# Probabilities times values with v's low part in the columns that held zeros

## The chip, the cores and the metric

The kernel runs on one core of a Trainium2 chip. The metric is the device time of one launch in microseconds. The engines in the profile are PE (matrix products; PEld is its weight load), DVE (vector), ACT (scalar), POOL and SP (which here issues DMAs).

## What is computed

Two layers of an encoder over 256 tokens of width 1024, one batch entry, float32. Each layer is a mixer with three kinds of attention heads of width 64 side by side, and then a gated feed-forward part:

```python
def mixer_sublayer(x, n1, w_in_l, qg, kg, rpb_l, og, w_out_l, tables):
    h = rms_norm(x, n1)
    proj = h @ w_in_l
    qa, ka, va, qd, kd, vd, qc, kc, vc = jnp.split(proj, cuts, axis=-1)
    ...                       # norms of q and k, rotations
    out_a = neighbourhood_attention(qa, ka, heads(va, H_NA), rpb_l, na_idx, na_dr, na_dc)   # 4 heads
    out_d = dilated_window_attention(qd, kd, heads(vd, H_DIL), dil_idx, dil_val)            # 6 heads
    out_c = gqa_block_attention(qc, kc, heads(vc, H_GKV))                                   # 6 heads on 2 of k, v
    mix = jnp.concatenate([rms_norm(out_a, og[:NA_W]), rms_norm(out_d, ...), rms_norm(out_c, ...)], axis=-1)
    return x + mix @ w_out_l

def channel_sublayer(x, n2, w_gu, cw, cb, w_dn):
    h = rms_norm(x, n2)
    g, u = jnp.split(h @ w_gu, 2, axis=-1)
    g = depthwise_conv_centred(g, cw, cb)
    return x + (jax.nn.gelu(g, approximate=False) * u) @ w_dn
```

The change is in the step of every attention that multiplies the probabilities, 256 queries by 256 keys, with the values v of the head.

## The kernel before

**Number format.** Every matrix product runs on float32r operands, which keep fewer digits than float32. So each operand is split: its high part is the rounded value, its low part the difference, and a product is the sum of three, high by high, high by low and low by high (`mm3`). For a weight, ACT writes `wp_hi` by a cast and DVE writes `wp_lo` by a subtraction, in chunks of 512 columns (`split`).

**Order of the work.** The program does not issue instructions as it is written. `Plan` records each operation with its tiles, `order()` puts them in one order with a list scheduler (an operation's start from its engine, its inputs and the buffer slots that it needs, by a table of costs and of handovers between engines; ties by the place in the program, shifted by `later`), and `emit()` issues them. So every instruction carries line 413 in the profile, and what is read are the names of the tiles. Each engine runs its own list in order. A changed operation changes the lists of all engines.

**Stages of a layer.** First come the norm and transposes of x (`act_hT`), then the projections into `psa` banks, split into seven pieces (`dq`, `dk`, `dv`, `cq`, `ckv`, `aqk`, `av`). The attention handles the heads in pairs: `scores` writes the scores of two heads, `softens` the softmax (DVE adds the bias and takes the maximum, ACT the exponential and the scaling), `turn` transposes the probabilities on PE and splits them into `act_ch` (high, by ACT) and `act_cl` (low, by DVE), and `weigh` multiplies them with v into a PSUM bank `psw_w`. `mixed` scales a finished pair into `act_mixT_hi` and `act_mixT_lo` and squares it into `act_sqm`; `group_rstd` turns the squares of a group of heads into the factor of its norm. The remaining projections, and the output projections of the groups that are ready, are a stock of products (`filler`) with which PE fills the waits of the attention. The output projections of the last group, of the residual into `const_x`, and the norm and transposes for the feed-forward part end the mixer. The feed-forward part is 11 steps of products with a fixed order.

**Values before.** Tiles `vown` and `vkv` exist twice, for v's high and low part. Each has the heads at odd places of 64 columns and zeros, written once by POOL, at the even places. The slice for a head is 128 columns, its own 64 and 64 zeros, before them or behind them by whether the head is even or odd (`beside_zeros`). So the product of a head gives 128 rows, of which the 64 of the other head of the pair are zero, and both heads of a pair are summed into one bank of 128 x 256: even heads in the lower 64 partitions, odd heads in the upper ones. Per head there are two key halves of three products:

```python
                for kt in range(NT):
                    mm3(
                        op, self.v[0][:, kt], self.v[1][:, kt], hi[:, kt], lo[:, kt],
                        first and kt == 0, last and kt == NT - 1,
                    )
```

`values_of` writes the high part with one ACT instruction and the low part with one DVE instruction per 128 tokens.

Of the kernel before, what the change touches and what calls it, by code (L numbers as in the profile page):

```python
# [455 lines left out]
def encoder_kernel(  # L456
# [70 lines left out]
    with nc.later(1000):  # L527
# [288 lines left out]
    for l in range(DEPTH):  # L816
# [163 lines left out]

        def values(places, src, t):

            hi, lo = places
# [4 lines left out]
        def values_of(tiles, ps, c0, t, nh):  # L988
            src = ps[:, c0 : c0 + nh * HD].rearrange("p (h d) -> p h d", d=HD)
            values([z[:, t, 1 : 2 * nh : 2] for z in tiles], src, t)  # L990

        def beside_zeros(tiles, h, odd):

            i = 2 * h + 1 - odd
            return [z[:, :, i : i + 2].rearrange("p t m d -> p t (m d)") for z in tiles]


        class Head:
# [103 lines left out]
        def prep_c(which, g):  # L1102
# [4 lines left out]
            for t in range(NT):  # L1107
# [4 lines left out]
                if which == "k":  # L1112
# [3 lines left out]
                    )  # L1116
                    values_of(vkv, ps, GKV_W, t, H_GKV)
                hold["c" + which, t] = z
# [50 lines left out]
        for h in range(H_DIL):  # L1169
            heads.append(Head("d", h, h, [dil[:, t] for t in range(NT)], beside_zeros(vown, h, h % 2)))  # L1170
        for h in range(H_GQ):
            kv = h // (H_GQ // H_GKV)
            heads.append(Head("c", h, kv, None, beside_zeros(vkv, kv, h % 2)))
        for h in range(H_NA):
            heads.append(Head("a", h, h, na_bias(h), beside_zeros(vown, h, h % 2)))

        def values_a():
            for t in range(NT):
                values_of(vown, pj["av"][t], 0, t, H_NA)
# [22 lines left out]
        for t in range(NT):  # L1202
            values_of(vown, pj["dv"][t], 0, t, H_DIL)
        wv.fill(1500)
# [241 lines left out]
```

## Time and profile before

| | before |
|---|---|
| time, median of 3 runs (lowest to highest) | 617.32 us (617.11 to 617.4) |
| profiled execution, span from first to last instruction | 615.5 us |
| busy share of the span: PE, DVE, ACT, POOL | 98%, 79%, 70%, 14% |
| value products (`act_ch` and `act_cl` by `const_v`) | 192 |
| additions and copies across partitions | none |

The page gives the profiled execution's span and no other time of it; the median of the runs lies 1.8 us above the span. A row of a group or of the timeline gives engine, operation, output tile, input tiles and shape; "x88 | 36.8, 422" means 88 instructions, 36.8 us busy together, 422 ns the mean of one. Durations of neighbours on an engine overlap, so the distance from start to start is often shorter than a duration. A number in brackets at the end of a timeline row is the idle time of the engine ahead of it, and what ended it.

### The profile page before, as it was taken

What the parts mean: (1) busy time and instruction counts of PE and PEld (TensorE: products, weight loads), DVE (VectorE), ACT (ScalarE), POOL (GpSimd) and SP (SyncE); (2) the same over time, 40 slices, a digit from 0 to 9 for tenths busy, and PEclk for the clock granted to TensorE, in tenths of its full rate; (3) what the DMA queues carried; (4) which work ended last, traced back from release to release, by engine and by line L of the source; (5) the groups of instructions that cost most, each with busy time, mean ns of one, the idle gap of its engine ahead of it and who ended that gap; (6) DMA issues with size and microseconds to landing.
All of it is one profiled execution on the core that took longest, in us unless ns stands there. A gap on an engine that the chain in (4) does not pass through costs nothing.

```text
span 615.5 us, 9869 instructions
## 1 busy us (share of the span) xinstructions
PE 604.9 (98%) x3484; PEld 523.7 (85%) x3484; DVE 486.9 (79%) x1000; ACT 428.3 (70%) x1064; POOL 84.0 (14%) x136
## 2 busy tenths in 40 slices
PE   8999999999999999999999999998999999999997
PEld 7998878888888888888899988887888888888885
DVE  4888989888778988878867797867877777777774
ACT  6888989686566677666588898866755656556651
POOL 2741230212400000000032213333000000000000
PEclk9999999999999999999999999999999999999999
DMA  8894313656596999988445644554565566555501
GB/s 287 275 291 143 102 35 104 208 192 195 164 252 235 364 353 325 309 278 269 154 150 173 222 137 171 205 175 135 179 231 171 176 204 205 166 180 201 185 21 68
DMA packets 85073, 121.44 MB, mean 197 GB/s; under 512 B 9864, under 2 KB 69608, under 8 KB 85024
## 3 DMA queue, kind: packets, MB, share of 16 engines
q1 hardware_dynamic: 82752, 112.17, 55.6%
q0 software_dynamic: 1728, 8.39, 4.0%
q8 instruction: 27, 0.44, 0.3%
q10 hardware_dynamic: 544, 0.26, 0.2%
q14 instruction: 22, 0.18, 0.1%
HBM read 110.93 MB, written 9.88 MB: 196 GB/s over the span
## 4 chain that ended last, share of the span: by engine, by line
PE 92%; DVE 3%; ACT 2%; issue 1%; DMA 1%; POOL 0%; SPq 0%; DVEq 0%; ACTq 0%
PE psw_w L413 49%; PE psa_a L413 43%; DVE const_x L413 1%; ACT act_s2k L413 1%; DVE wp_lo L413 1%; DMA wp_raw<-in_w_in_dram 1%; DVE act_hT L413 1%; ACT act_hT L413 1%; ACT wp_hi L413 1%; POOL small_rstd L413 0%; ACT act_mixT_hi L413 0%; POOL small_ms L413 0%; SPq L413 0%; DVE act_mixT_lo L413 0%; DVE small_ss L413 0%
## 5 line engine op out<-in xcount | busy, mean ns | idle before, releaser
L413 DVE TENSOR_TENSOR wp_lo<-wp_raw,wp_hi 128x512 fp32r<-128x512 f32 (+2 forms) x332 | 232.3, 731 | 42.9 <-ACT wp_hi L413 41.4
L413 PE MATMUL psw_w<-act_hT,wp_hi 128*128 128x512 f32 x704 | 247.8, 397 | 2.1 <-DVE act_hT L413 2.1
L413 ACT CAST wp_hi<-wp_raw 128x512 fp32r<-128x512 f32 (+2 forms) x332 | 203.1, 662 | 26.1 <-PE psw_w L413 15.3
L413 PE MATMUL psw_w<-act_hT,wp_lo 128*128 128x256 f32 x704 | 196.1, 279 | 0.1
L413 PEld LDWEIGHTS psw_w<-act_hT,wp_hi 128*128 128x128 f32 x704 | 131.9, 188 | 34.1 <-DVE act_hT L413 3.0
L413 PEld LDWEIGHTS psw_w<-act_hT,wp_lo 128*128 128x128 f32 x704 | 132.6, 188 | 1.5 <-DVE wp_lo L413 0.4
L413 PE MATMUL psa_a<-wp_hi,act_hT 128*128 128x384 f32 (+2 forms) x448 | 112.8, 332 | 0.7 <-ACT act_hT L413 0.5
L413 ACT COPY act_s2k<-psw_w 128x256 f32<-128x256 f32 x88 | 32.4, 373 | 76.3 <-PE psw_w L413 76.3
L413 PEld LDWEIGHTS psa_a<-wp_hi,act_hT 128*128 128x128 f32 x448 | 77.9, 189 | 3.8 <-ACT act_hT L413 1.0
L413 PE MATMUL psa_a<-wp_lo,act_hT 128*128 128x384 f32 (+2 forms) x224 | 74.7, 334 | 0.0
L413 PE MATMUL psa_a<-wp_lo,act_ch 128*128 128x512 f32 x176 | 69.5, 395 | 0.0
L413 PE MATMUL psa_a<-wp_hi,act_ch 128*128 128x512 f32 x176 | 69.4, 394 | 0.0
L413 PE MATMUL psa_a<-wp_hi,act_cl 128*128 128x512 f32 x176 | 65.8, 394 | 0.0
L413 DVE TENSOR_TENSOR act_s2k<-psw_w,act_s2k 128x256 f32<-128x256 f32 x88 | 36.8, 422 | 31.1 <-ACT act_s2k L413 30.7
L413 PEld LDWEIGHTS psa_a<-wp_lo,act_hT 128*128 128x128 f32 x224 | 42.3, 189 | 2.0 <-DVE wp_lo L413 1.0
L413 PEld LDWEIGHTS psa_a<-wp_hi,act_ch 128*128 128x128 f32 x176 | 33.1, 188 | 7.9
L413 PEld LDWEIGHTS psa_a<-wp_hi,act_cl 128*128 128x128 f32 x176 | 33.2, 188 | 7.8
L413 PEld LDWEIGHTS psa_a<-wp_lo,act_ch 128*128 128x128 f32 x176 | 33.1, 188 | 6.9
L413 DVE SCALAR_TENSOR_TENSOR act_s2k<-act_s2k,act_cw,act_s2k 128x255 f32<-128x255 f32 x88 | 36.9, 478 | 1.5 <-ACT act_s2k L413 1.3
L413 POOL TENSOR_TENSOR small_rstd<-small_ms,const_mh 128x6 f32<-128x6 f32 (+2 forms) x26 | 31.6, 1216 | 2.2
L413 ACT ACTIVATE act_s2k<-act_s2k,act_cw 128x256 f32<-128x256 f32 x44 | 24.1, 595 | 9.8 <-DVE act_s2k L413 9.4
L413 PE MATMUL psw_w<-act_ch,const_v 128*128 128x256 f32 x128 | 28.6, 286 | 1.1 <-ACT act_s2k L413 1.1
(112 smaller groups left out, 779.3 us busy)
## 6 DMA issues: line engine op xcount, KB each, us to landing
wp_raw<-in_w_gate_up_dram SPq DMA_DIRECT2D x44, 1024.0 KB, 5.1
wp_raw<-in_w_down_dram SPq DMA_DIRECT2D x22, 1024.0 KB, 4.8
wp_raw<-in_w_in_dram SPq DMA_DIRECT2D x14, 768.0 KB, 5.3
wp_raw<-in_w_in_dram SPq DMA_DIRECT2D x8, 1024.0 KB, 6.3
wp_raw<-in_w_out_dram SPq DMA_DIRECT2D x8, 768.0 KB, 6.4
dram_khi<-act_mixT_hi SPq DMA_DIRECT2D x4, 768.0 KB, 4.3
dram_klo<-act_mixT_lo SPq DMA_DIRECT2D x4, 768.0 KB, 5.6
wp_lo<-dram_klo POOLq DMA_DIRECT2D x4, 768.0 KB, 4.8
```

The lines of the kernel that those rows point to most:

```text
L413: getattr(o.engine.real, o.method)(*map(real, o.args), **{k: real(v) for k, v in o.kw.items()})
```

## The change

v's high and low part now stand side by side in one tile. In `vown` two heads take four places of 64 columns, high, low, low, high; an even head's slice is [high, low], an odd head's [low, high]. In `vkv` each of the two heads takes three places, high, low, high, so that a slice of either kind can be taken. One product of the probabilities' high part and one of their low part with the 128 columns then give the product with v's high part in one half of the partitions and that with v's low part in the other half. Two products per key half take the place of three; the product of low by low, which was left out, is now included. The two heads of a pair have a half bank of 256 columns each. `mixed` adds the halves: ACT copies the half that lies in the other 64 partitions to where it belongs (`act_mxs`), DVE adds it to the half that lies there already (`act_mxm`), for each head of the pair. What followed reads the sum from SBUF instead of the bank, and POOL takes the squares of all pairs of a group but the last. The low parts of `vown` are written with two DVE instructions instead of one, and the high part of `vkv` is written twice by one ACT instruction of double width. The zeros and their four memsets go.

```diff
-    vown, vkv = (
-        [const.tile([P, NT, 2 * n + 1, HD], F32R, tag=f"v{n}{i}", name=f"v{n}{i}") for i in range(2)]
-        for n in (H_DIL, H_GKV)
-    )
-    for z in vown + vkv:
-        nc.gpsimd.memset(z[:, :, 0::2].bitcast(F32), 0.0)
+    vown = const.tile([P, NT, 2 * H_DIL, HD], F32R, tag="vown", name="vown")
+    vkv = const.tile([P, NT, 3 * H_GKV, HD], F32R, tag="vkv", name="vkv")
...
+        def values_own(ps, t, nh):
+            z = vown[:, t, : 2 * nh].rearrange("p (h m) d -> p h m d", m=4)
+            hi, lo = z[:, :, 0:4:3], z[:, :, 1:3]
+            src = ps[:, : nh * HD].rearrange("p (h e d) -> p h e d", e=2, d=HD)
             r = rx[:, t : t + 1]
             nc.scalar.activation(hi, src, AF.Copy, scale=r)
-            nc.vector.scalar_tensor_tensor(lo, src, r, hi.bitcast(F32), ALU.mult, ALU.subtract)
+            for e in range(2):
+                nc.vector.scalar_tensor_tensor(
+                    lo[:, :, e], src[:, :, e], r, hi[:, :, e].bitcast(F32), ALU.mult, ALU.subtract
+                )
...
-            def weigh(self, op, first, last):
-                hi, lo = self.pT
+            def weigh(self, op):
                 for kt in range(NT):
-                    mm3(
-                        op, self.v[0][:, kt], self.v[1][:, kt], hi[:, kt], lo[:, kt],
-                        first and kt == 0, last and kt == NT - 1,
-                    )
+                    for i, z in enumerate(self.pT):
+                        nc.tensor.matmul(
+                            op, self.v[:, kt], z[:, kt],
+                            start=kt == 0 and i == 0, stop=kt == NT - 1 and i == 1,
+                        )
 
         def mixed(op, gi, i):
...
-            nc.scalar.activation(h, op, AF.Copy, scale=g)
-            nc.vector.scalar_tensor_tensor(mixT_lo[:, k], op, g, h.bitcast(F32), ALU.mult, ALU.subtract)
+            small_ = act.tile([P, S], F32, tag="mxs", name=f"mxs{gi}{l}{i}", bufs=1)
+            m = act.tile([P, S], F32, tag="mxm", name=f"mxm{gi}{l}{i}", bufs=2)
+            for e, (mine, other) in enumerate(((LOW, HIGH), (HIGH, LOW))):
+                nc.scalar.copy(small_[mine], op[other, e])
+            for e, mine in enumerate((LOW, HIGH)):
+                nc.vector.tensor_tensor(m[mine], op[mine, e], small_[mine], op=ALU.add)
+            nc.scalar.activation(h, m, AF.Copy, scale=g)
+            nc.vector.scalar_tensor_tensor(mixT_lo[:, k], m, g, h.bitcast(F32), ALU.mult, ALU.subtract)
             sq = act.tile([P, S], F32, tag="sqm", name=f"sqm{gi}{l}{i}", bufs=2)
-            nc.scalar.activation(sq, op, AF.Square)
+            if i < n - 1:
+                nc.gpsimd.tensor_tensor(sq, m, m, op=ALU.mult)
+            else:
+                nc.scalar.activation(sq, m, AF.Square)
...
         def weigh(i):
             gi, h = groups[i]
             if h % 2 == 0:
-                hold["op"] = psw.tile([P, S], F32, tag="w", name=f"o_{l}{i}")
-            heads[i].weigh(hold["op"], h % 2 == 0, h % 2 == 1)
+                hold["op"] = psw.tile([P, 2, S], F32, tag="w", name=f"o_{l}{i}")
+            heads[i].weigh(hold["op"][:, h % 2])
```

More of the change, by code (lines that the diff above doesn't have):

```diff
@@ L979, in by_pairs, with values_kv, both_parts @@
             return both
-        def values(places, src, t):
-            hi, lo = places
+        def values_own(ps, t, nh):
+            z = vown[:, t, : 2 * nh].rearrange("p (h m) d -> p h m d", m=4)
+            hi, lo = z[:, :, 0:4:3], z[:, :, 1:3]
+            src = ps[:, : nh * HD].rearrange("p (h e d) -> p h e d", e=2, d=HD)
             r = rx[:, t : t + 1]
             nc.scalar.activation(hi, src, AF.Copy, scale=r)
-            nc.vector.scalar_tensor_tensor(lo, src, r, hi.bitcast(F32), ALU.mult, ALU.subtract)
[L988 to L995, printed above, removed]
+            for e in range(2):
+                nc.vector.scalar_tensor_tensor(
+                    lo[:, :, e], src[:, :, e], r, hi[:, :, e].bitcast(F32), ALU.mult, ALU.subtract
+                )
+        def values_kv(ps, c0, t):
+            z = vkv[:, t].rearrange("p (h m) d -> p h m d", m=3)
+            src = ps[:, c0 : c0 + H_GKV * HD].rearrange("p (h d) -> p h d", d=HD)
+            r = rx[:, t : t + 1]
+            nc.scalar.activation(
+                z[:, :, 0:3:2], src.unsqueeze(2).to_broadcast([P, H_GKV, 2, HD]), AF.Copy, scale=r
+            )
+            nc.vector.scalar_tensor_tensor(z[:, :, 1], src, r, z[:, :, 0].bitcast(F32), ALU.mult, ALU.subtract)
+        def both_parts(z, i):
+            return z[:, :, i : i + 2].rearrange("p t m d -> p t (m d)")
         class Head:
@@ L1169, in encoder_kernel @@
         for h in range(H_DIL):
-            heads.append(Head("d", h, h, [dil[:, t] for t in range(NT)], beside_zeros(vown, h, h % 2)))
+            heads.append(Head("d", h, h, [dil[:, t] for t in range(NT)], both_parts(vown, 2 * h)))
         for h in range(H_GQ):
             kv = h // (H_GQ // H_GKV)
-            heads.append(Head("c", h, kv, None, beside_zeros(vkv, kv, h % 2)))
+            heads.append(Head("c", h, kv, None, both_parts(vkv, 3 * kv + h % 2)))
         for h in range(H_NA):
-            heads.append(Head("a", h, h, na_bias(h), beside_zeros(vown, h, h % 2)))
+            heads.append(Head("a", h, h, na_bias(h), both_parts(vown, 2 * h)))
         def values_a():
             for t in range(NT):
-                values_of(vown, pj["av"][t], 0, t, H_NA)
+                values_own(pj["av"][t], t, H_NA)
         groups = [(gi, h) for gi, n in enumerate((H_DIL, H_GQ, H_NA)) for h in range(n)]
@@ L1202, in encoder_kernel @@
         for t in range(NT):
-            values_of(vown, pj["dv"][t], 0, t, H_DIL)
+            values_own(pj["dv"][t], t, H_DIL)
         wv.fill(1500)
```

3 lines of the change are left out of this document (2 added, 1 removed).

## Prediction

> **What bounds the kernel now.** I read the first part of the page, then the windows cut at the stages, then the timeline of one stretch of probability-times-value products, then the groups by form, and the chain of waits for the seams between stages.
>
> ```profile
> span 615.5 us, 9869 instructions
> PE 604.9 (98%) x3484; PEld 523.7 (85%) x3484; DVE 486.9 (79%) x1000; ACT 428.3 (70%) x1064; POOL 84.0 (14%) x136
> PE 92%; DVE 3%; ACT 2%; issue 1%; DMA 1%; POOL 0%; SPq 0%; DVEq 0%; ACTq 0%
> ```
>
> PE is busy nearly throughout and carries 92% of the chain that ended last, so a matmul taken out should be time won. But shares over the whole span hide stages. In the next view the columns are PE, PEld, DVE, ACT and POOL busy (instructions), granted clock, DMA share, GB/s. The first two rows are layer 0 from the first scores to the last value product, and from there to the feed-forward part; the fourth and fifth are the same two stages of layer 1.
>
> ```profile
> 45.00:114.50 69.50, 68.01 (x491) 59.51 (x491) 62.03 (x175) 61.27 (x181) 15.01 (x20) 1.00 0.32 107
> 114.50:127.70 13.20, 12.07 (x65) 9.42 (x63) 11.35 (x22) 10.67 (x26) 4.31 (x6) 1.00 0.54 172
> 127.70:311.60 183.90, 183.89 (x971) 156.78 (x972) 151.56 (x258) 120.61 (x225) 9.52 (x18) 1.00 0.79 261
> 346.70:412.30 65.60, 65.04 (x479) 57.38 (x479) 52.76 (x159) 55.78 (x168) 19.07 (x29) 1.00 0.48 164
> 412.30:429.10 16.80, 15.11 (x78) 11.90 (x76) 11.81 (x22) 10.35 (x26) 4.87 (x8) 1.00 0.39 131
> ```
>
> The change touches the first, second, fourth and fifth rows only. The feed-forward stages are PE alone. In the attention of layer 0, DVE is busy 62.03/69.50 = 89% and ACT 88%; in layer 1, 80% and 85%. PE is kept full there because projection and output-projection products fill the waits of the softmax; those fillers are a fixed stock. The clock is 1.00 everywhere and stays out of the sum.
>
> **What it removes.** Each head goes from six products of 256 columns to four; 16 heads and two layers make 192 into 128. The timeline of PE gives the distance from one to the next:
>
> ```profile
> 101.92 0.40 PE L413 MATMUL psw_w<-act_ch,const_v 128*128 128x256 f32 x2
> 102.15 0.28 PE L413 MATMUL psw_w<-act_cl,const_v 128*128 128x256 f32 x1
> 102.27 0.40 PE L413 MATMUL psw_w<-act_ch,const_v 128*128 128x256 f32 x2
> 102.50 0.28 PE L413 MATMUL psw_w<-act_cl,const_v 128*128 128x256 f32 x1
> 102.62 0.40 PE L413 MATMUL psw_w<-act_ch,const_v 128*128 128x256 f32 x2
> 102.86 0.28 PE L413 MATMUL psw_w<-act_cl,const_v 128*128 128x256 f32 x1
> 102.98 0.28 PE L413 MATMUL psw_w<-act_ch,const_v 128*128 128x256 f32 x1
> ```
>
> Nine products start between 101.92 and 102.98: 1.06/9 = 0.118 us each (the 0.28 us of one is overlapped). 64 x 0.118 = 7.55 us off PE, 3.8 a layer, with their weight loads inside. The four memsets of zeros on POOL go too, in the first microseconds, with nobody waiting for them: nothing.
>
> **What it adds.** For each of eight pairs of heads a layer: two ACT copies and two DVE additions of 64x256, since one half of the result lies in the other 64 partitions. No row has 64 partitions; the nearest are the same operations on 128.
>
> ```profile
> L413 DVE TENSOR_TENSOR act_s2k<-psw_w,act_s2k 128x256 f32<-128x256 f32 x88 | 36.8, 422 | 31.1 <-ACT act_s2k L413 30.7
> L413 ACT COPY act_s2k<-psw_w 128x256 f32<-128x256 f32 x88 | 32.4, 373 | 76.3 <-PE psw_w L413 76.3
> L413 ACT ACTIVATE act_sqm<-psw_w 128x256 f32<-128x256 f32 x16 | 6.2, 388 | 0.0
> L413 DVE SCALAR_TENSOR_TENSOR const_v<-psa_a,small_rx,const_v 128x384 fp32r<-128x384 f32 x4 | 2.4, 612 | 0.5 <-ACT const_v L413 0.5
> L413 DVE SCALAR_TENSOR_TENSOR const_v<-psa_a,small_rx,const_v 128x256 fp32r<-128x256 f32 x4 | 1.7, 471 | 0.0
> L413 DVE SCALAR_TENSOR_TENSOR const_v<-psa_a,small_rx,const_v 128x128 fp32r<-128x128 f32 x4 | 1.3, 345 | 0.0
> 96.58 0.42 DVE L413 CUSTOM_DVE_ANT_0 act_s2k<-psw_w,act_nab 128x256 f32<-128x256 f32 x1
> 96.92 0.42 DVE L413 CUSTOM_DVE_ANT_0 act_s2k<-psw_w,act_nab 128x256 f32<-128x256 f32 x1
> ```
>
> An addition costs DVE between 0.34 (the two custom operations of the same width start 96.58 and 96.92) and 36.8/88 = 0.42 us. The values' low part is written in two instructions for one, four more a layer: two of 128 columns for one of 256 are 2 x 345 - 471 = 0.22 us more, and 384 split in two about the same by interpolation, 0.9 a layer at most, 0.5 if the ends overlap. DVE gains 16 x 0.34 + 0.5 = 5.9 to 16 x 0.42 + 0.9 = 7.6 us a layer. I take 6.7, the middle, since DVE queues are full there but not always. ACT gains 16 x 32.4/88 = 5.9 and loses five squares of 0.39 to POOL: 4.0 net, and some 0.3 for writing the grouped values' high part twice. POOL gets five squares a layer; its sum of squares over two tiles takes 0.74, and POOL is idle three quarters of the stage. The low part of the mixed result is computed from SBUF rather than PSUM, at the same width: nothing.
>
> **Where it lies, layer 0.** The PE gain would shorten the 69.5 us to 65.7. DVE then has 62.0 + 6.7 = 68.7 us of work for it, which doesn't fit. At 69.5 us unchanged it would be 99% full. What allows that at all is that part of its 7.5 us idle is stall that ends: the mixed low part waits for ACT's square on the same PSUM bank, which the new order of reads removes for most pairs.
>
> ```profile
> L413 DVE SCALAR_TENSOR_TENSOR act_mixT_lo<-psw_w,const_gains,act_mixT_hi 128x256 fp32r<-128x256 f32 x16 | 7.6, 476 | 4.3 <-ACT act_sqm L413 3.0 <-ACT act_mixT_hi L413 1.3
> 114.54 0.48 ACT L413 ACTIVATE act_mixT_hi<-psw_w,const_gains 128x256 fp32r<-128x256 f32 x1 [2.26 <-PE psw_w L413]
> 117.49 0.72 POOL L413 TENSOR_SCALAR small_ms<-small_ss 128x2 f32<-128x2 f32 x1 [1.38 <-DVE small_ss L413]
> ```
>
> Against it stand the new waits: an addition waits for ACT's copy, and behind it on DVE stand low parts of weights and of turned probabilities (act_cl), which PE's fillers and value products wait for. So I put the attention of layer 0 at no change, DVE having taken over from PE as what ends last. The seam behind it (114.5 to 127.7) is a chain from the last product over mixed result, squares, group norm, residual, transposes to the feed-forward part; before its 114.54 now come two copies and two additions, 2 x 0.37 + 2 x 0.42 = 1.6 us with every handover on top, less what overlaps (the second copy runs under the first addition): 1.3. In the changed kernel's PE order 25 output-projection products stand behind the last value product, for 29 before, so PE is no longer what fills it. DVE's wait for POOL and the weight splits in that seam can take half of the 1.3: +0.6 for layer 0.
>
> **Layer 1.** Here the order says the most: 23 such products stand behind the last value product, for 41. Their distance is read off the chain of waits:
>
> ```profile
> 412.35 3.97 PE psa_a L413 x17
> ```
>
> 3.97/17 = 0.234 us, so 18 x 0.234 = 4.2 us of filler have moved from the seam into the attention, in place of the 3.8 removed. The attention stays at 65.6 us, with DVE at 52.8 + 6.7 = 59.5 (91%), and the seam shrinks: not by 4.2, since the chain that took 13.2 us in layer 0, now 1.3 longer, bounds it at 14.5: 16.8 - 14.5 = 2.3 gained.
>
> Sum: +0.6 - 2.3 = -1.7 us, made on the profiled span, 615.5 to 613.8. The page gives no other time for that execution; the median of the runs shown, 617.32, is 1.8 above the span, and I keep that difference: 615.6.
>
> **A rule against it.** POOL's new squares read SBUF while DVE subtracts weights in SBUF. The trace has the case:
>
> ```profile
> 83.31 0.73 POOL L413 TENSOR_TENSOR act_sqm<-act_sqm,act_sqm 128x256 f32<-128x256 f32 x1
> 83.65 0.68 DVE L413 TENSOR_TENSOR act_z<-act_z,act_gna 128x256 f32<-128x256 f32 x1
> 85.90 0.41 DVE L413 TENSOR_TENSOR act_z<-act_z,act_gna 128x256 f32<-128x256 f32 x1
> ```
>
> The same operation takes 0.68 under POOL's and 0.41 alone: 0.27 us for each square that meets one, 1.4 a layer at most; it is priced in the slower rival. [...]
>
> **Rivals.** (1) *Held additions.* If a DVE instruction that starts at the other 64 partitions lets the one before it drain, the addition on the upper half and the instruction behind it each lose the overlap of 0.42 - 0.34 = 0.08 us: two instructions for each of eight pairs, 16 x 0.08 = 1.3 us in layer 0, where DVE is the bound, and hidden in layer 1: 616.9. No row has a start at another partition, for or against. [...]
>
> (2) *DVE bounds layer 0 outright: slower.* It runs in order and waits for ACT, PE and POOL. The fullest stretch of over ten microseconds that I found is early in layer 1's attention:
>
> ```profile
> 353.30:366.00 12.70, 12.70 (x85) 10.67 (x86) 11.99 (x37) 11.96 (x33) 1.94 (x4) 1.00 0.36 115
> ```
>
> That is 11.99/12.70 = 94%. With the work of 68.7 and 1.4 of contention at that share, the stage takes 74.6, 5.1 us more; with the seam's +0.6 to 1.3 and layer 1's -2.3, +3.4 to 4.1: about 621. It decides from the share where the loss in layer 0 eats the 2.3, that is 70.1/(69.5 + 1.7) = 98% with contention, 96% without. For it: both DVE and ACT near 90%, in-order queues, only one filler product of the four early units left at the end of layer 0. Against: the square's stall goes, and DVE's queue holds weight splits that fill its waits.
>
> (3) *PE stays the bound in both layers: the full gain.* DVE additions at 0.34, seams covered: 617.3 - 7.5 + 1.2 for two seams = 611.0. For it: 98% PE. Against: 62.0 + 5.9 in 65.7 us is 103%.
>
> That the change does not do what it says I set aside: the built order has 64 fewer products on PE, 32 additions on DVE and 32 copies on ACT more.
>
> **How the numbers follow.** The forecast, 615.6 with its own range 613.5 to 617, gets 0.38; (1) 616.9, 0.15; (2) 621, 0.31; (3) 611, 0.16. Range 610.8 to 621.5: from the full gain to (2) with a margin for its share. What a measurement here can tell from no change is 0.2%, 1.2 us: faster means under 616.1, slower over 618.6. Faster: 0.31 of the forecast, 0.16 of (3), 0.01 of (1) = 0.48. Same: 0.07 + 0.11 = 0.18. Slower: 0.31 + 0.03 = 0.34.
>
> **What would show it.** Right: the 128x256 value products 128 with 0.118 between them; DVE over 95% in the attention of layer 0, PE with new idle there released by DVE or ACT; the seam of layer 1 two microseconds shorter, that of layer 0 not. An addition under 0.34 or over 0.45 breaks the price. Wrong: PE idle of several microseconds in layer 0's attention (rival 2), or both attentions 3 us shorter (rival 3).

## The result, and the profile after

The changed kernel takes 627.25 us (median of 4 runs, 625.93 to 627.67), the kernel before beside it 617.36 us (617.11 to 618.11): the ratio is 1.0158, 95% interval 1.0146 to 1.0171. It is 9.9 us slower, where 1.7 us faster was forecast. The profiled execution has a span of 625.2 us, 9.7 above that of before, so the traces can be compared stage by stage. First the head of the page after: span, engines, and the chain that ended last.

```profile
span 625.2 us, 9798 instructions
PE 606.1 (97%) x3420; PEld 517.1 (83%) x3420; DVE 502.7 (80%) x1040; ACT 439.9 (70%) x1086; POOL 92.4 (15%) x142
PE 82%; DVE 7%; ACT 7%; POOL 2%; issue 1%; ACTq 0%; POOLq 0%
```

PE has 64 instructions fewer and carries ten points less of the chain; DVE and ACT carry 14% of it instead of 5%. DVE gained 15.8 us of work and ACT 11.6. The windows cut at the same stages as before: attention and seam of layer 0, its feed-forward part, attention and seam of layer 1. The columns are PE, PEld, DVE, ACT and POOL busy (instructions), granted clock, DMA share, GB/s.

```profile
45.10:119.60 74.50, 70.36 (x463) 57.63 (x463) 67.70 (x190) 66.22 (x190) 19.23 (x26) 0.98 0.30 100
119.60:135.90 16.30, 12.22 (x62) 8.51 (x60) 15.15 (x29) 12.51 (x30) 6.24 (x6) 1.00 0.48 171
135.90:319.80 183.90, 183.90 (x971) 156.74 (x972) 150.67 (x256) 119.58 (x223) 10.95 (x19) 1.00 0.78 259
354.80:423.90 69.10, 67.11 (x465) 56.76 (x465) 59.68 (x177) 60.36 (x177) 23.66 (x36) 1.00 0.49 168
423.90:438.80 14.90, 11.12 (x60) 8.28 (x59) 11.45 (x23) 11.31 (x28) 4.18 (x6) 1.00 0.31 97
```

The feed-forward row is the same to a tenth. The attention of layer 0 went from 69.5 to 74.5 us and its seam from 13.2 to 16.3; the attention of layer 1 from 65.6 to 69.1 and its seam from 16.8 to 14.9. That is +5.0, +3.1, +3.5 and -1.9, together +9.7: all of the difference. The 0.98 in the first row is a stretch of 3.4 us in which PE had half its clock (last section); that can be up to some 1.7 of the 5.0. PE's longest waits from the start of layer 0's attention to the end of its seam (engine, what it waited for, us in total, times, longest) name DVE and ACT. First all of the kernel before, then the four longest of the changed one, whose waits there sum to 7.9 us:

```profile
PE psw_w L413 <- ACT act_s2k L413: 1.1, 1, 1.1
PE psw_w L413 <- DVE act_mixT_lo L413: 0.4, 1, 0.4
```

```profile
PE psw_w L413 <- DVE act_hT L413: 2.5, 2, 1.4
PE psw_w L413 <- ACT act_s2k L413: 1.6, 2, 0.8
PE psw_w L413 <- DVE const_x L413: 1.3, 2, 1.0
PE psa_a L413 <- DVE wp_lo L413: 1.1, 3, 0.6
```

The groups show what the added operations cost:

```profile
L413 DVE TENSOR_TENSOR act_mxm<-psw_w,act_mxs 64x256 f32<-64x256 f32 x32 | 13.4, 418 | 2.6 <-ACT act_mxs L413 2.2
L413 ACT COPY act_mxs<-psw_w 64x256 f32<-64x256 f32 x32 | 11.8, 367 | 7.5 <-PE psw_w L413 6.6 <-DVE act_mxm L413 0.3
L413 DVE SCALAR_TENSOR_TENSOR act_mixT_lo<-act_mxm,const_gains,act_mixT_hi 128x256 fp32r<-128x256 f32 x16 | 8.1, 509 | 2.8 <-ACT act_mixT_hi L413 2.8
L413 POOL TENSOR_TENSOR act_sqm<-act_mxm 128x256 f32<-128x256 f32 x10 | 6.8, 676 | 36.3 <-DVE act_mxm L413 36.3
```

An addition took 0.418 us and a copy 0.367, both as priced. The mixed result's low part took 0.509 instead of 0.476. So the single prices held. Their sum was too small: over the whole kernel DVE gained 15.8 us of busy time where 13.4 were forecast, ACT 11.6 where 8.6 were. The next sections show that the place where they fall was read wrong as well.

### The profile page after: what moved, and what is told of

Read it like the earlier page. It is cut to its first block, busy times and chain, and to the rows that moved or that the text cites. A ratio compares the mean times of both kernels' runs of the same rounds, so it can differ in the third digit from the quotient of the medians.

```text
span 625.2 us, 9798 instructions
## 1 busy us (share of the span) xinstructions
PE 606.1 (97%) x3420; PEld 517.1 (83%) x3420; DVE 502.7 (80%) x1040; ACT 439.9 (70%) x1086; POOL 92.4 (15%) x142
## 4 chain that ended last, share of the span: by engine, by line
PE 82%; DVE 7%; ACT 7%; POOL 2%; issue 1%; ACTq 0%; POOLq 0%
PE psw_w L413 46%; PE psa_a L413 37%; ACT act_s2k L413 3%; DVE wp_lo L413 2%; ACT wp_hi L413 1%; POOL small_rstd L413 1%; DVE const_x L413 1%; DVE act_mxm L413 1%; ACT act_mxs L413 1%; DVE act_cl L413 1%; ACT act_hT L413 1%; DVE act_mixT_lo L413 1%; DVE small_nm L413 1%; ACT act_ch L413 0%; DVE small_ss L413 0%
## 5 line engine op out<-in xcount | busy, mean ns | idle before, releaser
L413 PE MATMUL psa_a<-wp_lo,act_ch 128*128 128x512 f32 x176 | 69.5, 395 | 0.0
L413 POOL TENSOR_TENSOR small_s1x<-small_ssx 128x2 f32<-128x2 f32 x4 | 4.9, 1218 | 176.6 <-ACT act_s2k L413 176.6
```

Source lines behind the costliest of these rows:

```text
L413: getattr(o.engine.real, o.method)(*map(real, o.args), **{k: real(v) for k, v in o.kw.items()})
```

## The experiments

Times below are medians; a ratio is against the kernel before beside it, with its 95% interval. A difference between two changed kernels is worked out from their ratios, times 617.4 us, with the two half-widths added in squares. Most of these kernels have stretches of 3.4 us in which PE had half its clock (last section), and not the same number in each execution. In the profiled executions a mean granted clock of 0.999 or 1.00 goes with none in the stages that matter (the kernel before has 1.000), 0.997 with one (the changed kernel) and 0.994 with two (the kernel with one more ACT copy); for the executions without a profile the number is estimated from their mean clock in the same way. Where it decides a reading, executions of equal clock are compared as well; that is one to six executions on a side.

The first theory was that the copies and additions load DVE and ACT beyond what the attention can hide; its rival that the order which the scheduler writes anew for the shorter products loses the time. The first four kernels split the change.

**The products alone.** The bank of a pair is used as it stands; copies, additions and POOL's squares go.

```diff
-            ...                                        # two copies, two additions
+            m = op[:, 0]
-            if i < n - 1:
-                nc.gpsimd.tensor_tensor(sq, m, m, op=ALU.mult)
-            else:
-                nc.scalar.activation(sq, m, AF.Square)
+            nc.scalar.activation(sq, m, AF.Square)
```

> Leaves out the copies and additions of the halves: the mixed result is read from one head's half bank, as the kernel before reads its bank, with ACT's squares; the two products per key half stay. If the additions are the whole loss (theory D: DVE, and ACT with it, bound layer 0 and the seams), the PE gain comes through: 64 x 0.118 = 7.5 us less than before, about 610 to 612. If the fixed stock of fillers hides PE's gain anyway (theory F), 615 to 617. If something of the new value layout or of the rewritten order costs by itself (theory O), 617 or more.

Measured 615.25 us, ratio 0.9978 (0.9966 to 0.9990): 1.4 us faster. 7.5 us of work left PE and 1.4 arrived; in the six of ten executions without a stretch at half clock, 615.1 us, it was 2.3.

**The copies and additions alone**, put into the mixed step of the kernel before, with its three products and zeros. POOL's squares come with them.

```diff
-            nc.scalar.activation(h, op, AF.Copy, scale=g)
-            nc.vector.scalar_tensor_tensor(mixT_lo[:, k], op, g, h.bitcast(F32), ALU.mult, ALU.subtract)
...
+            for e, (mine, other) in enumerate(((LOW, HIGH), (HIGH, LOW))):
+                nc.scalar.copy(small_[mine], op[other])
+            for e, mine in enumerate((LOW, HIGH)):
+                nc.vector.tensor_tensor(m[mine], op[mine], small_[mine], op=ALU.add)
+            nc.scalar.activation(h, m, AF.Copy, scale=g)
+            nc.vector.scalar_tensor_tensor(mixT_lo[:, k], m, g, h.bitcast(F32), ALU.mult, ALU.subtract)
...
```

> The kernel before, three products and zeros, with the changed kernel's copies, additions and POOL squares put in its mixed step (it adds the other head's rows to each, so the sum is not the reference's). Theory D: the loss is that of the additions, and PE was no longer the bound in layer 0, so taking the products away bought little: 628 to 632. If the gain of 7.5 was won in full and merely outweighed (theory S, plain sum of +17 and -7.5): 634 to 636.

Measured 629.38 us, 1.0198 (1.0181 to 1.0215): 12.2 us slower. With the additions present, going from three products to two is worth 2.5 us (629.38 to the changed kernel, by the ratios); without them 1.4. So two things are to be explained: why additions of 0.42 us cost 12 us, and why 7.5 us off PE are worth so little in either case.

**Additions and copies over all 128 partitions**, so that no instruction starts at another partition than the one before it. The order of instructions is the changed kernel's on every engine; the values are not, since each half bank is added to its own copy.

```diff
-            for e, (mine, other) in enumerate(((LOW, HIGH), (HIGH, LOW))):
-                nc.scalar.copy(small_[mine], op[other, e])
-            for e, mine in enumerate((LOW, HIGH)):
-                nc.vector.tensor_tensor(m[mine], op[mine, e], small_[mine], op=ALU.add)
+            for e in range(2):
+                nc.scalar.copy(small_[:, e], op[:, e])
+            for e in range(2):
+                nc.vector.tensor_tensor(m2[:, e], op[:, e], small_[:, e], op=ALU.add)
```

> The changed kernel with copies and additions of the same number and the same 256 columns, but over all 128 partitions of each half bank, so that no instruction starts at another partition than its neighbours (the sum of a half with its own copy, not with the other half). Theory Hd (an addition at the upper 64 partitions and its successor are held until DVE has drained): neighbouring additions start 0.34 apart instead of 0.43 to 0.46, DVE has 16 x 0.1 = 1.6 us less a layer, and the time falls by 1.5 to 3 us, to 624 to 626. If holding costs nothing, 627.

Measured 623.16 us, 1.0091 (1.0073 to 1.0108): 4.1 us (2.8 to 5.4) less than the changed kernel. The timelines of DVE and of ACT, changed kernel first, then this one, show the same pair of additions and the same pair of copies:

```profile
71.68 0.86 DVE L413 TENSOR_TENSOR act_mxm<-psw_w,act_mxs 64x256 f32<-64x256 f32 x2
70.90 0.75 ACT L413 COPY act_mxs<-psw_w 64x256 f32<-64x256 f32 x2
```

```profile
70.82 0.74 DVE L413 TENSOR_TENSOR act_mxm<-psw_w,act_mxs 128x256 f32<-128x256 f32 x2
70.02 0.65 ACT L413 COPY act_mxs<-psw_w 128x256 f32<-128x256 f32 x2
```

With 0.42 us for one, the second starts 0.43 us after the first in the changed kernel, when that has ended, and 0.32 after it here, 0.10 before its end. Where the two additions of a pair stand apart in the changed kernel, the rows show that it is the start that holds, and not the 64 partitions:

```profile
84.32 0.40 DVE L413 TENSOR_TENSOR act_mxm<-psw_w,act_mxs 64x256 f32<-64x256 f32 x1
84.64 0.41 DVE L413 TENSOR_TENSOR act_z<-act_z,act_gna 128x256 f32<-128x256 f32 x1
85.08 0.43 DVE L413 TENSOR_TENSOR act_mxm<-psw_w,act_mxs 64x256 f32<-64x256 f32 x1
85.54 0.69 DVE L413 TENSOR_TENSOR act_cl<-psw_w,act_ch 128x512 fp32r<-128x512 f32 x1
```

Behind the lower addition, the first of a pair, the next instruction starts after 0.32 us, 0.08 before its end. The upper one starts 0.44 us behind an instruction of 0.41, and what follows it 0.46 us later, where it takes 0.43: both start 0.03 us behind the end of the one before, both are held. ACT shows the same: with 0.37 us for one copy, the second starts 0.38 us after the first in the changed kernel, and 0.27 after it here, where one takes 0.38. So the 4.1 us are what holding costs on DVE and ACT together, and this experiment does not part the two. A little of it is the clock: at equal clock the difference is 3.5 to 3.9.

**The squares back on ACT.**

```diff
-            if i < n - 1:
-                nc.gpsimd.tensor_tensor(sq, m, m, op=ALU.mult)
-            else:
-                nc.scalar.activation(sq, m, AF.Square)
+            nc.scalar.activation(sq, m, AF.Square)
```

> The changed kernel with all squares on ACT. Theory P (POOL's squares slow DVE's subtractions in SBUF and are slowed by them, 0.3 to 0.5 each): 1 to 3 us faster, 624 to 626. If ACT, 89% busy in layer 0, is what bounds, ten more squares of 0.31 make it 1 to 3 us slower, 628 to 630.

Measured 629.44 us, 1.0203 (1.0179 to 1.0226), 2.8 us (1.2 to 4.4) more than the changed kernel: ten squares on ACT cost more than what DVE may lose beside POOL's squares (in the kernel before one DVE operation took 0.68 us beside a sum of squares and 0.41 alone). What DVE loses to them over the kernel is not measured by itself. Of the 2.8, some is the clock: the four executions have 0.989 to 0.997, and the one at 0.997 is 1.2 longer than the changed kernel at 0.997.

Next, one suspect at a time. **Without the copies**, the additions read a table in SBUF as their second input, so the other half is left out; **without the additions**, the copies write the mixed input directly, with the same omission.

```diff
-                nc.scalar.copy(small_[mine], op[other, e])
...
+                nc.vector.tensor_tensor(
+                    two(m[mine]), two(op[mine, e]), gains_of["rot"][mine, :, 0:P], op=ALU.add
+                )
```

> The changed kernel without ACT's copies: the additions take a table in SBUF as their second input, on the same partitions, so they stay, two of 64 partitions a pair, held as before (the low part of v is left out of the sum). Theory D (DVE's work, 32 additions and what they hold, is the loss): little changes, 625 to 627. Theory A (ACT's 32 copies of 0.37 are the loss, ACT being 89% busy in layer 0): 619 to 621. Theory L (the longer chain from product to mixed result in the seams, not the load): about 1 us off each seam, 625.

```diff
-                nc.scalar.copy(small_[mine], op[other, e])
-            for e, mine in enumerate((LOW, HIGH)):
-                nc.vector.tensor_tensor(m[mine], op[mine, e], small_[mine], op=ALU.add)
+                nc.scalar.copy(m[mine], op[other, e])
```

> The changed kernel without DVE's additions: ACT's copies write the mixed result directly (v's high part is left out). Theory D: most of the ten to twelve microseconds that the additions cost comes back, 617 to 619, near the kernel without copies and additions (615.3). Theory A: 623 to 626.

Measured 621.77 us, 1.0069 (1.0054 to 1.0084), and 622.55 us, 1.0081 (1.0064 to 1.0098): 5.5 and 4.8 us less than the changed kernel (5.0 to 5.5 and 3.4 at equal clock). Neither of the two is the cause alone; each costs about half. Both kernels also have a shorter chain from the product to the mixed result and an order written anew, so that they do not show by themselves whether the load or the chain costs.

**The scheduler told** that an addition on 64 partitions takes 90 units longer in its table of costs; the instructions are the same.

```diff
+        if method == "tensor_tensor" and out.shape[0] < P:
+            n += 90
```

> The changed kernel with one figure of the scheduler's cost table changed: an addition of fewer than 128 partitions is put down as 94 ns longer, which is what the rows show (0.43 between two such additions where the table has 0.34). The instructions are the same, their order is made for their real length. Theory O (the order, made for additions that were too short, loses what it could keep): 2 to 4 us faster, 623 to 625. If the order does not matter, 626 to 628.

Measured 625.83 us, 1.0143 (1.0120 to 1.0165): 0.9 us less, with an interval of 1.6 on either side; nothing that this comparison can tell.

**One more instruction per pair, off the chain**: a DVE addition, and in another kernel an ACT copy, of 128x256 into a tile that nobody reads.

```diff
+            nc.vector.tensor_tensor(junk, m, dil[:, 0], op=ALU.add)     # the first kernel
+            nc.scalar.copy(junk, m)                                     # the second
```

> The changed kernel with one more DVE addition of 128 partitions per pair into a tile that nobody reads: 16 in all, 0.34 to 0.42 each, 3 us a layer, off every chain. Theory D, with DVE the bound in layer 0's attention and seam: 3 us more from layer 0 and some from layer 1, 630 to 632. If what counts is the longer chain and not DVE's load: 627 to 628.

> The changed kernel with one more ACT copy of 128x256 from SBUF per pair into a tile that nobody reads, off every chain, 16 in all of about 0.31: 2.5 us a layer. If DVE alone bounds the attention (theory D in its narrow form): 627 to 628. If ACT paces it as much as DVE does (as the kernel without copies, 5.5 us faster, says): 629 to 632.

```profile
L413 DVE TENSOR_TENSOR act_mxj<-act_mxm,const_dil 128x256 f32<-128x256 f32 x16 | 8.3, 518 | 0.1
```

```profile
L413 ACT COPY act_mxj<-act_mxm 128x256 f32<-128x256 f32 x16 | 6.5, 404 | 4.2 <-DVE act_mxm L413 4.2
```

Measured 630.50 us, 1.0214 (1.0198 to 1.0230), and 629.93 us, 1.0198 (1.0175 to 1.0220): 3.5 (2.2 to 4.7) and 2.5 us (0.9 to 4.1) more than the changed kernel, for work that nothing waits for. Durations of neighbours overlap; the engine's busy time grew by 6.9 us on DVE (502.7 to 509.6) and by 4.4 on ACT (439.9 to 444.3). That is 0.5 and 0.6 us for each microsecond added; at equal clock it is 2.7 for 6.9, and 1.5 to 2.8 for 4.4, so 0.3 to 0.6. And this although in the changed kernel neither engine is over 91% busy in any stage but the seam. The order is written anew in both, which by the two kernels with a changed table of costs (the one above, and the changed kernel told one and a half times the price below) is worth about a microsecond. The kernel with whole-bank additions has no such doubt: at an unchanged order it has 3.1 us less on DVE and 3.9 less on ACT, and is 3.5 to 4.1 us shorter, 0.5 or 0.6 for one. At 0.3 to 0.6 the 15.0 us of DVE and 10.7 of ACT that the kernel with copies and additions alone has over the one before make 8 to 15 us: an estimate, with the 12.2 measured inside it.

**The mixing placed at once** among ready instructions instead of later.

```diff
-SPLIT_LATER, TURN_LATER, MIX_LATER, PREP_LATER, KEEP_LATER = 50, 100, 100, 30, 100
+SPLIT_LATER, TURN_LATER, MIX_LATER, PREP_LATER, KEEP_LATER = 50, 100, 0, 30, 100
```

> The changed kernel with the scheduler's shift for the mixed step set from 100 to 0, so that copies and additions go before other work that is ready at the same time: the same instructions in another order. It shows what the order alone is worth: if the loss is load on DVE and ACT, 626 to 629; if the additions come too late for the output projections and the squares (theory L), 622 to 625.

Measured 628.76 us, 1.0188 (1.0173 to 1.0203): 1.9 us slower than the changed kernel. Its executions have a mean clock of 0.991 to 0.995, for 0.997 in three of the changed kernel's four, so the difference can be the clock's. As it stands, to mix sooner won nothing.

Now the other question, what became of the products' 7.5 us. **The order of before on every engine, without the products with v's low part** (that part of the values is left out; 64 products go).

```diff
+                if o.method == "matmul" and o.args[1].tile in self.left_out:
+                    continue
```

> The kernel before with its order kept instruction for instruction on every engine, but the products with v's low part not issued: four of six a head, 64 fewer, with zeros, values and mixed step as they are (v's low part is left out of the sum). If PE is the bound at every place (98% busy): 7.5 us less, 610. If the attention is paced by the chain of softmax and splits through DVE and ACT, and PE's share of it is filled with a fixed stock of products (theory F), PE idles where the products were: 614 to 616, like the kernel without additions (615.3), and then the rewritten order of that kernel is not what hid the gain. If the rewritten order hid it (theory O): 610 to 612.

Measured 611.75 us, 0.9911 (0.9896 to 0.9926): 5.5 us faster, and the fastest kernel of the study. The windows of its two attentions are 66.55 and 62.85 us, 2.95 and 2.75 less than before; the third row is the seam of layer 1, 16.65 for 16.80:

```profile
45.30:111.85 66.55, 65.05 (x459) 55.53 (x459) 60.71 (x175) 61.01 (x181) 14.98 (x20) 1.00 0.35 111
344.00:406.85 62.85, 62.05 (x447) 53.66 (x447) 52.34 (x159) 55.42 (x168) 19.05 (x29) 1.00 0.51 170
406.85:423.50 16.65, 15.06 (x76) 11.83 (x75) 11.76 (x22) 10.28 (x26) 4.78 (x8) 1.00 0.39 131
```

The same 64 products are worth 5.5 us at a fixed order and 1.4 (2.3 without half clock) where the order is written anew. Three of the next four kernels change only what the scheduler is told of a value product's price, the fourth only the products at a fixed order.

```diff
-        return n / (2.4 if args[1].dtype == F32R else 1.2) + 2.5, 0
+        f = 1.5 if args[1].tile in VALUES else 1.0          # 2 / 3 for the kernel before
+        return f * (n / (2.4 if args[1].dtype == F32R else 1.2) + 2.5), 0
```

**Two products without additions, told one and a half times the price:**

> The kernel of two products without copies and additions (615.25 us), with the scheduler told that a value product takes one and a half times as long. As there, the result is read from one head's half of the bank, so the other half's sum is left out. If the order written anew is what hid the gain of the products, 611 to 612.5, as with the fixed order (611.75). If the gain is lost for another reason, 615, and 616 or more if the order does not suit.

Measured 612.55 us, 0.9928 (0.9913 to 0.9942): 3.1 us (1.9 to 4.3) less than at the true price, near the fixed order; at equal clock 2.2. **The kernel before, told two thirds of the price:**

> The kernel before, with all three products, and the scheduler told that a value product takes two thirds of its time; nothing but the order differs. If an order planned for short heads costs by itself what the fixed order points to, 620 to 621. If it costs nothing, 617 to 618.

Measured 622.58 us, 1.0099 (1.0071 to 1.0128): the order alone, with all the instructions of before, costs 6.1 us, its stretches at half clock included (mean clock 0.994 to 0.998). The windows of layer 1 show how. First the products alone at the true price, then told one and a half times, then the kernel before told two thirds; attention and seam of each:

```profile
345.72:415.87 70.15, 68.25 (x469) 59.06 (x468) 54.13 (x163) 55.90 (x168) 20.12 (x31) 0.98 0.50 168
415.87:429.53 13.66, 10.20 (x54) 7.52 (x54) 10.70 (x21) 10.51 (x26) 4.21 (x6) 1.00 0.42 143
```

```profile
344.97:407.85 62.88, 62.16 (x447) 53.59 (x447) 52.63 (x161) 55.50 (x168) 19.08 (x29) 1.00 0.50 171
407.85:424.56 16.71, 15.01 (x76) 11.79 (x75) 11.79 (x22) 10.32 (x26) 4.82 (x8) 1.00 0.39 131
```

```profile
347.97:419.29 71.32, 69.57 (x498) 61.17 (x498) 54.22 (x161) 55.86 (x168) 20.15 (x31) 1.00 0.49 163
419.29:434.40 15.11, 12.27 (x57) 9.32 (x57) 10.97 (x21) 10.90 (x26) 3.69 (x6) 0.89 0.40 137
```

When the scheduler thinks a head short, it puts some twenty output-projection products that stood in the seam into the attention (18 and 22 are left behind the last value product, for 41 before and with the price one and a half times). In the kernel before told two thirds, the attention grows by 5.7 us, and the seam, which is a chain through ACT, DVE and POOL, shrinks by only 1.7; up to 1.7 of these net 4.0 is the half clock in its seam (0.89). With two products, attention and seam together take 79.6 us with the seam full and 83.8 with it emptied, again with one stretch at half clock in the second (0.98).

**The changed kernel, told one and a half times the price:**

> The changed kernel, instruction for instruction, but the scheduler that writes the order is told that a value product takes one and a half times as long, so that it plans for a head as it did with three products. Nothing but the order differs. If the order that is written for the short heads loses some 3.5 us (the theory from the fixed order: 5.9 us for the products there, 2.1 with the order written anew), 623 to 625. If the loss is the load of the copies and additions alone, 627 as the changed kernel, within 1 us. If the order written for the true price was the better one, 628 or more.

Measured 625.68 us, 1.0140 (1.0125 to 1.0155): 1.1 us less, give or take 1.2, and 0.4 at equal clock. With the additions present the order is worth little in sum. But it moves time between the stages: here layer 0's attention takes 71.55 us at full clock, with DVE at 67.42/71.55 = 94%, and layer 1's takes 70.80. **The additions and three products, in that order, without the products of v's low part:**

> Three products with the zeros, the copies and the additions (629.38 us), in its order on every engine, but the products with the low part of v are not issued, so that this part of the values is left out. If TensorE still sets the pace there, the gain is that without additions, 5.5 to 6 us: 623.5. If the copies and additions have made VectorE and ScalarE the bound of the attention, the gain is under 2 us: 627.5 to 629.

Measured 626.72 us, 1.0155 (1.0138 to 1.0172): 2.7 us (1.2 to 4.2) less than with the products, where the same products at a fixed order were worth 5.5 without additions. The attentions, first with three products, then without those of the low part:

```profile
44.75:118.75 74.00, 71.31 (x495) 60.12 (x495) 67.13 (x186) 65.91 (x190) 18.92 (x25) 1.00 0.31 101
354.20:425.40 71.20, 69.74 (x495) 59.82 (x495) 59.23 (x174) 60.06 (x177) 23.18 (x36) 1.00 0.48 163
```

```profile
45.50:119.00 73.50, 69.62 (x463) 57.88 (x463) 66.96 (x186) 66.04 (x190) 18.98 (x25) 0.98 0.31 101
354.50:423.40 68.90, 67.28 (x463) 55.19 (x463) 59.05 (x174) 59.94 (x177) 22.93 (x36) 1.00 0.50 168
```

In layer 1, 2.3 of 2.75 us arrives. In layer 0 only 0.5 of some 3 does, with DVE at 91% and ACT at 90%, but up to 1.7 us of the missing part may be the half clock that the second fence's first row shows (0.98); all four executions of this kernel have it (0.996 or 0.997), and three of four with the products have not. So in layer 1 PE still is for the most part what ends last. In layer 0 it is left open by this pair how much of the gain arrives, between 0.5 and 2.2 us.

Taken together, for the 9.8 us: with an order that suits, two products without additions stand at 612.55 us and with them at 625.68, so copies and additions cost 13.1 us (11.8 to 14.4). The products are worth 4.4 to 5.5 us against before. What the order adds in the changed kernel is 1.1 us and not told from nothing; where no additions are present it is 3.1 (2.2 at equal clock). Without the copies on ACT 5.5 us come back, without the additions on DVE 4.8; within these, the holding of both engines at the change of partitions is 4.1 (3.5 to 3.9 at equal clock). That time on the two engines costs time of the kernel is shown by the whole-bank additions at an unchanged order, and the extra instructions bear it out; how much of the 13.1 us is such load and how much the longer chain of the seams is not parted. No two-product kernel with additions came near the one before. The kernel at 611.75 us beats both, at the price of v's low part, which is another computation than this change was to make.

## Why the prediction was wrong

**Prices: right one by one, too low in sum.** The product was put at 0.118 us; in the changed kernel two that stand back to back start at 114.49 and 114.61:

```profile
114.49 0.29 PE L413 MATMUL psw_w<-act_ch,const_vown 128*128 128x256 f32 x1
114.61 0.29 PE L413 MATMUL psw_w<-act_cl,const_vown 128*128 128x256 f32 x1
```

The addition was put at 0.34 to 0.42 and the copy at 0.37; 0.418 and 0.367 are measured. But the full 7.5 us never came, at the best order 5.5: a price from a stretch in which products stand back to back overstates what the stage gives back. And what the engines gain was put too low in sum, 6.7 us a layer on DVE for 7.9, 4.3 on ACT for 5.8.

**Layer 0's attention "at no change": the step that failed.** It was put at 69.5 us, on the ground that DVE would be 99% full there and that the ending of the square's stall allowed it. The stall did end (over the kernel the mixed low part waits 2.8 us in place of 4.3, and for `act_mixT_hi` alone), but the additions wait 2.6 us instead, and the stage took 74.50 us with DVE at 67.70/74.50 = 91%. In no kernel of this study was DVE over 95% busy in this stage. Rival (2) had worked out 74.6 us for the stage; that the number agrees is in part luck. It came from 70.1 us of work at a share of 94%, where 67.70 were measured at 91%, and up to 1.7 us of the 74.50 is the half clock. Its share is the better part: with the order told one and a half times, the same instructions run in 71.55 us at 94%, and with the additions over all partitions the stage has 67.62/71.40 = 95%:

```profile
45.20:116.60 71.40, 68.72 (x463) 56.10 (x463) 67.62 (x192) 64.40 (x190) 19.23 (x26) 1.00 0.32 104
```

So the step took an engine that runs in order, and waits for others, to be fillable to the brim. Nor was DVE alone the bound: ACT stands at 89% beside it, and instructions added to either, for which nobody waits, cost time.

**Layer 1's attention "stays at 65.6": also wrong,** at 69.10. DVE at 59.68/69.10 = 86% and ACT at 87% looked harmless share by share. Besides, the count of moved products was right (23 behind the last value product, for 41), and its reading was not: 4.2 us of filler in place of 3.8 us of products was taken as even, with the emptied seam a gain of 2.3. The seam did shrink by 1.9, as the bound of 14.5 said (14.90). But the same move in the kernel before, with the scheduler told two thirds of the price, lengthened the attention by 5.7 and shortened the seam by 1.7. The reading that fits is that the seam's chain is there in any case, so that products in it are hidden; in the attention they are not.

**Layer 0's seam: +0.6 forecast, +3.1 measured.** The chain of waits of the changed kernel in that place (start, us, engine, output):

```profile
120.98 0.43 DVE act_mxm L413
121.44 0.75 DVE const_x L413
122.19 0.60 DVE wp_lo L413
122.79 0.88 DVE act_mixT_lo L413
124.19 0.68 DVE wp_lo L413
125.29 0.73 POOL small_ms L413
126.09 1.04 POOL small_rstd L413
127.16 2.07 DVE const_x L413 x4
```

`small_ms` starts at 125.29. From the last product's end at the cut, 119.60, that is 5.7 us; in the kernel before it started at 117.49, 3.0 after the cut at 114.50. So 2.7 of the 3.1 us are there. POOL's sum of the squares parts them, in the kernel before and then in the changed one:

```profile
115.37 0.74 POOL L413 TENSOR_TENSOR act_sqm<-act_sqm,act_sqm 128x256 f32<-128x256 f32 x1 [6.14 <-ACT act_sqm L413]
122.54 0.84 POOL L413 TENSOR_TENSOR act_sqm<-act_sqm,act_sqm 128x256 f32<-128x256 f32 x1 [4.54 <-ACT act_sqm L413]
```

It starts 2.9 us after the cut instead of 0.9: 2.1 of the 2.7 are the two copies and two additions ahead of it (119.60 to 121.41) and what follows them on ACT. The forecast had added these up to 1.6, taken off 0.3 for overlap, and half of the rest as hidden; nothing of it was. The other 0.6 lie behind the sum, where DVE does the mixed low part and two weights' low parts before `small_ss`, the reduction for which `small_ms` waits.

**Rival (1), held additions: right as a mechanism,** and under-priced: 4.1 us, or 3.5 to 3.9 at equal clock, for 1.3. It was an assumption there; that additions are held is shown by the rows of the changed kernel and of the one with additions over all partitions, 0.43 for 0.32 us from the one to the next. The rival knew it on DVE alone; ACT's copies are held as well, and that is part of the 4.1. And it was counted in layer 0 alone and taken as hidden in layer 1, whose attention and seam together are 1.5 us shorter without it (82.5 us for 84.0, both at full clock).

**Rival (3), the full PE gain, and POOL's squares.** No kernel with additions shows (3); without additions and at a suitable order it holds to 5.5 of 7.5 us. A square's sum on POOL takes 0.884 us in the mean for 0.736 before. In the changed kernel the two DVE subtractions for `wp_lo` that run beside POOL's square at 101.62 and its sum at 102.41 take 1.10 and 1.14 us, where the 224 of that shape have a mean of 0.693; the one at 112.33, beside another sum, takes 0.68. What this costs the kernel is not measured, only that the squares on ACT cost more.

## What to carry to other kernels

Where two engines are both near 90% busy in a pipelined stage, don't ask which of them has room: price each microsecond that is added to either at a good part of a microsecond (here 0.3 to 0.6), and try one idle instruction on the chip to learn the rate. When a list scheduler writes the order, separate an edit's work from the order that it provokes, by running the new work in the old order and the old work in the new one: here the order cost 3 to 6 us by itself where PE was the bound, stretches at half clock included. And filler that is hidden behind a chain is worth most where the chain is: here some twenty products moved out of it cost 5.7 us and saved 1.7, one stretch at half clock included. Last, where the clock differs between executions, compare those of equal clock before a difference of two microseconds is given a cause.

## What the runs showed of the hardware

The clock was taken to be 1.00 throughout. In several kernels it wasn't: PE had a clock of 0.50 for 3.4 us. The windows before, in and after such a stretch of the changed kernel:

```profile
64.90:68.30 3.40, 2.10 (x13) 1.43 (x12) 3.34 (x14) 3.40 (x12) 0.61 (x1) 1.00 0.01 2
68.30:71.70 3.40, 3.40 (x13) 3.01 (x13) 2.84 (x7) 2.71 (x9) 0.00 (x0) 0.50 0.24 78
71.70:75.10 3.40, 3.40 (x28) 2.74 (x28) 3.21 (x8) 2.57 (x7) 1.85 (x2) 1.00 0.40 154
```

PE was 2.10/3.40 = 62% busy in the 3.4 us ahead of it. Products of 512 columns start 0.43 us apart in the stretch (71.06 and 71.49) and 0.23 behind it (74.28 and 74.51); at 0.50 of the clock the 3.4 us cost PE some 1.7, an estimate. The products alone were executed ten times: six with a mean clock of 0.999 took 614.84 to 615.26 us, four with 0.997 took 616.71 to 617.75, some 2.2 us more. What brings a stretch about is not shown: in the same trace a later window of the same length was less busy, 1.90/3.41 = 56%, and the clock behind it stayed at 1.00.

```profile
126.33:129.74 3.41, 1.90 (x11) 0.99 (x9) 2.81 (x5) 3.00 (x8) 0.80 (x1) 1.00 1.01 384
129.74:133.15 3.41, 2.21 (x12) 1.94 (x13) 3.41 (x8) 3.30 (x9) 1.07 (x1) 1.00 0.05 19
```

In its profiled execution the kernel before has no such stretch before its last microseconds. By the mean clocks (0.999 and 0.997 of the products alone), the same kernel gets a stretch in one execution and none in the next, so a difference of a microsecond or two between medians can be the clock's; the mean clock of each execution tells, and the comparisons at equal clock above go by it.

A second thing is on record here: in the changed kernel the addition and the copy that start at the other 64 partitions than the one before them start when that one has ended, on DVE 0.43 us from start to start, for 0.32 where both start at the same partition, and on ACT 0.38 for 0.27.
